# Where the two heads of a pair meet on TensorE: SSD products by head, or by pair of heads

## The chip, the cores and the metric

The kernel runs on one core of a Trainium2 chip. The metric is the device time of one execution in microseconds (us), as the median over runs. Three runs of the kernel before gave 815.00, 816.15 and 816.83 us, median 816.15 us.

## The reference

Two layers of a bidirectional hybrid encoder over 256 tokens of 1024 features, in float32. A layer projects the normalized input to the columns of two mixers: a Mamba-2 mixer (SSD, 16 heads of 64 features in 4 groups, two chunks of 128 tokens, run forward and backward) and a short gated convolution. Both outputs go through one output projection; then comes a gated MLP. The part that matters here is the chunked scan, once for each direction:

```python
scores = jnp.einsum('bclgn,bcsgn->bclsg', cm, bm)
y_diag = jnp.einsum('bclsgr,bcsgrp->bclgrp', scores[..., None] * decay_ls, xdt)
...
y_off = jnp.einsum('bclgn,bcgrpn->bclgrp', cm, h_prev) * jnp.exp(a_cs)[..., None]
return (y_diag + y_off).reshape(bsz, length, g, r, p)
```

`y_diag` is what each chunk adds to itself, head by head: a 128 x 128 matrix of weights times 64 features. `y_off` is what one chunk hands to the other.

## The kernel before

**Work and tiles.** All activations lie with 128 features on the partitions and 256 tokens along the row. A large weight matrix comes as a stream of 512 KB chunks (`issue`, L132): SyncE loads a chunk into `raw`, ScalarE rounds it to `wh` (L98), VectorE takes the rest as `wl` (L99), seven buffers each, four chunks ahead of use. `products` (L230) spends 24 TensorE products on a chunk: for four k tiles and two column tiles, weights times input in three parts. These products are the rows `mm<-nh,wh`, `mm<-nl,wh`, `mm<-nh,wl` of the trace (`mm<-mixh,wh` and so on in the output projection).

**The order on TensorE** is the order written in the code: the class `te` (L79) ties every product to the one before it. In a mixer's second half, `mixer` runs over twelve pairs of tiles of the short convolution's projection, `TRIPLES` (24 chunks), and then over the 16 chunks of the output projection, `OUT_ORDER`. Between chunks it slips in the work of the SSD. The chunks are counted as slots: n from 1 to 39. `HEADS_AT` (L47) says after which slot a head is begun: heads 0 to 15 after slots 1, 3, 3, 7, 9, 11, 11, 15, 17, 19, 19, 21, 21, 23, 24, 24.

**A head** (`head`, L471) is begun by ScalarE and VectorE, which make its 128 x 128 weights for both chunks, the tile `m` (five buffers, written last by VectorE at L487). `HEAD_LAG` = 4 slots later `products_of` (L544) is called through `run` (L538) and issues the head's products through `head_out` (L492):

- the head's own products, `py<-m,xt`: one for each chunk c, of the 64 columns of `xt` that belong to the head. An even head writes partitions 0 to 63 of the bank `py`, an odd head partitions 64 to 127. In the trace each of these float32 products is two rows, so a head has four;
- with an even head also `py<-so,xg`, one for each chunk, over all 128 columns, for both heads of the pair: four rows.

After an odd head VectorE takes the bank `py` out (L554 to L557: `yo`, then twice the tile `x`). After every fourth head the group is gated, squared and, four slots later, its norm is taken with one product `gt<-sq,ones` (`group_norm`, L566). Before the first head of a group, `group` (L445) issues four transposes `xp<-ident,x` and two products `sp<-C,B` (four rows each).

The rows of decays that a pair needs (`bc`, `er`) are fetched on GpSimd's queue (`load_rows`, L573). Banks `py`, `xp`, `sp`, `gt` share four PSUM buffers (`bank`, L175).

Of the kernel before, what the change touches and what calls it, by code (L numbers as in the profile page):

```python
# [16 lines left out]
P = 128  # L17
L = 256
# [11 lines left out]
# per-feature parameter columns: name -> (first column, columns)  # L30
# [7 lines left out]
# pairs of 128-column tiles of the input projection, in the order they are used  # L38
# [6 lines left out]
# heads of the SSD begun after a chunk of products, counted from the short conv's first  # L45
_STARTS = (1, 3, 3, 7, 9, 11, 11, 15, 17, 19, 19, 21, 21, 23, 24, 24)
HEADS_AT = {_n: _STARTS.count(_n) for _n in _STARTS}  # L47
HEAD_LAG = 4    # chunks from a head's weights to its products
NORM_LAG = 4    # chunks from a group's last products to its norm
ROWS_AHEAD = 2  # heads whose rows are fetched ahead  # L50
STAGES_AT = (3, 5, 7, 9)    # pairs of SILUS after which a stage of the discretisation follows
SPLIT_FROM = 7  # triple after which the outputs of the mixers are split
NORMS = {"n1": D, "n2": D, "fin": D, "gn": 2 * P}     # features under each mean
NU = 4           # pairs of a projection whose input is scaled by rstd only afterwards
LNEXP, SILU = "natural_log_exp_and_others", "silu_and_others"
AHEAD = 4        # chunks of weights split ahead of their use
WARM = 12       # products that raise the clock of TensorE
LAG = 6         # tiles of d_ff between the up and the down projection
TAIL = 4        # tiles of d_ff whose down projection runs output by output
# [3 lines left out]
def hybrid_trunk(ctx: ExitStack, tc: tile.TileContext, xT, w_in, w_dt, w_out, w_up, w_dn, w_dnt,  # L63
# [15 lines left out]
    class te:  # L79
        """TensorE in the order written here"""  # L80
# [51 lines left out]
    def issue(halves=1, between=lambda: None):  # L132
        src, kc, cols = plan[len(split)]
        n = kc * cols
        raw = wp.tile([P, KC * 256], F32, name="raw")
        wh = wp.tile([P, KC * 256], F32R, name="wh", bufs=7)
        if cols == 32:
            # both parts of a k tile side by side
            nc.sync.dma_start(out=raw[:, :n], in_=src)
            r3 = raw[:, :n].rearrange("p (k c) -> p k c", k=kc)  # L140
            w4 = wh[:, :2 * n].rearrange("p (k i c) -> p k i c", k=kc, i=2)
            hilo(r3, w4[:, :, 0, :], w4[:, :, 1, :])
            split.append((wh, None, kc, cols))
            return
        wl = wp.tile([P, KC * 256], F32R, name="wl", bufs=7)
        for i in range(halves):
            o = slice(i * n // halves, (i + 1) * n // halves)
            nc.sync.dma_start(out=raw[:, o], in_=src[:, o])
            hilo(raw[:, o], wh[:, o], wl[:, o])
            if i == 0:  # L150
                between()
        split.append((wh, wl, kc, cols))
# [44 lines left out]
    # TensorE's clock is raised while the first loads are under way  # L197
# [18 lines left out]
    def scaled(l):  # L216
        """the norms' weights over -2n, a power of two"""
        for i, (name, n) in enumerate(NORMS.items()):
            a = s.activation(wn[l][:, i], pars[l][:, COL[name]:COL[name] + 8], AF.Identity, scale=-0.5 / n)
            if l:  # L220
                after(a, tab["uses"][-1])
# [8 lines left out]
    def products(ps, wts, xs, first, last, js=None):  # L230
        """ps[:, j, :] += w[k, j]^T x[k] for the k of a chunk."""
        wh, wl, kc, cols = wts
        for kk in range(kc):
            xh, xl = xs[kk]
            for j in js or range(cols // P):
                o = kk * cols + j * P
                a, b = wh[:, o:o + P], wl[:, o:o + P]
                f = first and kk == 0
                e = last and kk == kc - 1
                te.matmul(ps[:, j, :], a, xh, start=f and j == 0, stop=False, skip_group_check=True)  # L240
                te.matmul(ps[:, j, :], a, xl, start=False, stop=False, skip_group_check=True)
                te.matmul(ps[:, j, :], b, xh, start=False, stop=e, skip_group_check=True)
# [10 lines left out]
    def squares(p, src, acc):  # L253
        """acc of the squares of the four pairs of h."""
# [13 lines left out]
    def rstd(sq, n, name, sq_on):  # L268
        """-2n / sqrt(mean + eps) over the features of a tile of squares, on all partitions"""
# [5 lines left out]
    def newton(tot, n, y, t, r, sq_on=s):  # L275
        """-2n / sqrt(tot/n + eps): the tables' value, and one step of Newton's"""
# [10 lines left out]
    def weighted(l, name):  # L287
        """h * w in two parts, pair by pair; the scaling by rstd follows the product."""
# [22 lines left out]
    def both(r):  # L311
        """[128, L] seen twice as [128, 2, L]"""
        return bass.AP(r.tensor, r.offset, [r.ap[0], [0, 2], r.ap[1]])

    class Norm:
        """The normalized input of a projection: h*w first, (h*w)*rstd once rstd is known."""
# [24 lines left out]
        def pairs(self, extra=None):  # L341
            """pair by pair; rstd is due after the first chunk of the second"""
# [19 lines left out]
    def discretise(l, nm):  # L362
        """softplus, decays and their prefix and suffix sums, rows of (chunk, head); then per token. In stages."""
# [49 lines left out]
        # what is left of the chunk after s (forward, chunk 0) and before s (backward, chunk 1)  # L413
        keep(s.activation(rows[1][64:96, :], cs[qd[0], :], AF.Identity, scale=-1.0, bias=cs[qd[0], P - 1:P]))
        keep(s.activation(rows[1][96:128, :], rs[qd[1], :], AF.Identity, scale=-1.0, bias=rs[qd[1], 0:1]))
        # the rows that every partition needs go through DRAM: [head, (cs forward, rs backward), token]
# [10 lines left out]
        # what a token adds to the other chunk: dt * exp(rest), [128, chunk, head]  # L427
# [6 lines left out]
        # the decay from the other chunk up to l: rows of chunk 0 (backward), of chunk 1 (forward)  # L434
# [8 lines left out]
    def diag(t):  # L443
        """of [128, 2 L] the blocks of the two chunks with themselves: [128, 2, 128]"""
        return bass.AP(t.tensor, t.offset, [t.ap[0], [3 * P, 2], [1, P]])  # L445
# [23 lines left out]
    def head(hd, bc, tok, grp):  # L469
# [10 lines left out]
        # of the two exponents the one that applies is not positive and the other not negative  # L480
# [9 lines left out]
    def head_out(hd, grp, m, py):  # L490
        """of two heads, what each chunk adds to itself, and to the other chunk without the decay up to l"""
        xt, _, so, xg = grp  # L492
        i, f = hd % 2, hd % HPG
        for c in range(2):
            te.matmul(py[64 * i:64 * i + 64, 0, c * P:(c + 1) * P], xt[:, c * L + f * 64:c * L + (f + 1) * 64],
                      m[:, c, :], start=True, stop=True, skip_group_check=True)
        if i == 0:
            for c in range(2):
                te.matmul(py[:, 1, (1 - c) * P:(2 - c) * P], xg[:, c, f:f + 2, :].rearrange("p f x -> p (f x)"),
                          so[:, c, :], start=True, stop=True, skip_group_check=True)  # L500

    def mixer(l):
# [35 lines left out]
        def run(slot):  # L538
            """what is due after a block of products of the projections"""
# [4 lines left out]
        def products_of(hd, grp, m):  # L544
            def f(slot):
                if hd % 2 == 0:
                    state["py"] = bank("py")
                py = state["py"]
                head_out(hd, grp, m, py)
                g, j = hd // HPG, (hd % HPG) // 2  # L550
                if hd % 2 == 1:
                    t = k1("yo")
                    er = state["er"].pop(0)
                    v.tensor_tensor(out=t, in0=py[:, 1, :], in1=er, op=ALU.mult)  # L554
                    v.scalar_tensor_tensor(out=xs[g][:, j, :], in0=xs[g][:, j, :], scalar=pc(l, "dsk", 2 * g + j),
                                           in1=py[:, 0, :], op0=ALU.mult, op1=ALU.add)
                    v.tensor_tensor(out=xs[g][:, j, :], in0=xs[g][:, j, :], in1=t, op=ALU.add)  # L557
# [15 lines left out]
        def load_rows(upto):  # L573
            """the rows of the next heads on all partitions, and of the pairs of heads on 64 partitions each"""
# [22 lines left out]
        def split_next():  # L597
            """the parts of the next tiles of the mixers' outputs that are ready, those first used first"""
# [7 lines left out]
        state.update(ready=[], rows=0, bc=[], er=[])  # L606
# [89 lines left out]
    final = {"turn": [], "hw": []}  # L696

    def turned(p):
        """h * w of a pair with the tokens on partitions: two pairs to a bank"""
# [31 lines left out]
# (output pair, quarter of K); the quarters run over the short-conv half first  # L731
# [3 lines left out]
# the down projection of a tile of d_ff LAG tiles behind its up projection  # L735
# [6 lines left out]
def _pairs(w, kt):  # L742
    """[K, 256 n] columns -> [n, 128, kt*256]: k on partitions, k tiles along the row."""
# [4 lines left out]
def _chunks(w, kt):  # L748
    """the same cut into chunks of KC k tiles: [n, kt/KC, 128, KC*256]"""
# [4 lines left out]
def _feat(a):  # L754
    """[..., n*128] -> [128, ... n] columns"""
# [50 lines left out]
```

## Time and profile before

| | |
|---|---|
| median of three runs | 816.15 us (815.00 to 816.83) |
| profiled execution, first to last instruction (span) | 813.0 us |
| TensorE busy in the span | 803.1 us (99%) |
| VectorE, ScalarE, GpSimd busy | 648.6 us (80%), 530.9 us (65%), 39.4 us (5%) |
| mean granted TensorE clock | 0.997 |
| mean DMA rate | 186 GB/s |

The profile gives the span alone as the profiled execution's own time: 813.0 us, which is 3.15 us under the median of the runs. Busy shares are averages over stages. The heads of the first layer lie between 95 and 190 us, those of the second between 490 and 585 us. In the rows, PE is TensorE's products, PEld its weight loads, DVE is VectorE, ACT is ScalarE, POOL is GpSimd. `128*64` in a row means 128 rows and 64 columns of the array.

### The profile page before, as it was taken

The numbers are of one execution on the slowest core, as the hardware profiler recorded it, in microseconds if no ns is written. First come the engines' busy times: TensorE is split into PE (matmuls) and PEld (weight loads), VectorE is DVE, ScalarE is ACT, GpSimd is POOL, SyncE is SP. The second block draws the span as 40 slices with busy tenths as digits, with TensorE's granted clock in tenths as the row PEclk, the third lists the DMA queues.
The fourth block names the chain that finished last, engine by engine and source line by source line (L and its number), as shares of the span: only waits on it lengthen the run. The fifth ranks groups of instructions, "written<-read, shape, count | busy, mean of one in ns | idle before, by whom it ended". The sixth has DMA issues, their size and how long they took to land.

```text
span 813.0 us, 16585 instructions
## 1 busy us (share of the span) xinstructions
PE 803.1 (99%) x6608; PEld 792.7 (98%) x6608; DVE 648.6 (80%) x1082; ACT 530.9 (65%) x940; POOL 39.4 (5%) x68
## 2 busy tenths in 40 slices
PE   8999999999999999999999999999999999999996
PEld 8999999999999999999999999999999999999996
DVE  6998788988799877776789768899878987767753
ACT  6777867974676555555667578789557655555543
POOL 1002211100000000000000202110000000000000
PEclk9999999999999999999999999999999999999998
DMA  8578667546536855554546767645564566656511
GB/s 277 185 241 289 177 233 210 182 123 221 181 115 179 252 182 184 181 183 162 183 154 190 232 225 215 206 157 181 172 195 154 151 208 216 183 183 182 184 44 52
DMA packets 46989, 150.89 MB, mean 186 GB/s; under 512 B 9136, under 2 KB 9712, under 8 KB 46912
## 3 DMA queue, kind: packets, MB, share of 16 engines
q1 hardware_dynamic: 38880, 138.17, 53.6%
q0 software_dynamic: 7456, 11.00, 4.5%
q8 instruction: 51, 0.84, 0.4%
q10 hardware_dynamic: 576, 0.68, 0.2%
q14 instruction: 26, 0.21, 0.1%
HBM read 148.62 MB, written 1.15 MB: 184 GB/s over the span
## 4 chain that ended last, share of the span: by engine, by line
PE 98%; DVE 1%; DMA 1%; ACT 0%; issue 0%; DVEq 0%; POOLq 0%
PE mm L91 76%; PE dn L91 16%; PE py L91 3%; PE sp L91 1%; DMA hp<-in_hpar_dram 1%; PE dtp L91 0%; PE xp L95 0%; PE gt L91 0%; DVE hwl L295 0%; PE tot L91 0%; PE mm L95 0%; DVE fo L726 0%; DVEq L802 0%; ACT sq L256 0%; ACT wh L98 0%
## 5 line engine op out<-in xcount | busy, mean ns | idle before, releaser
L98 ACT CAST wh<-raw 128x1024 fp32r<-128x1024 f32 (+1 forms) x264 | 272.5, 1035 | 228.0 <-PE mm L91 145.2
L99 DVE TENSOR_TENSOR wl<-raw,wh 128x1024 fp32r<-128x1024 f32 (+1 forms) x262 | 317.2, 1213 | 110.6 <-ACT wh L98 110.3
L91 PE MATMUL mm<-nh,wh 128*128 128x256 f32 x1216 | 346.6, 285 | 0.0
L91 PE MATMUL mm<-nl,wh 128*128 128x256 f32 x1216 | 344.0, 283 | 0.0
L91 PE MATMUL mm<-nh,wl 128*128 128x256 f32 x1216 | 344.0, 283 | 0.0
L91 PEld LDWEIGHTS mm<-nh,wh 128*128 128x128 f32 x1216 | 233.3, 192 | 0.9 <-issue 0.7
L91 PEld LDWEIGHTS mm<-nl,wh 128*128 128x128 f32 x1216 | 233.3, 192 | 0.2
L91 PEld LDWEIGHTS mm<-nh,wl 128*128 128x128 f32 x1216 | 233.3, 192 | 0.0
L91 PE MATMUL dn<-acth,wh 128*128 128x256 f32 x352 | 99.7, 283 | 0.0
L91 PE MATMUL dn<-acth,wl 128*128 128x256 f32 x352 | 99.6, 283 | 0.0
L91 PE MATMUL dn<-actl,wh 128*128 128x256 f32 x352 | 99.6, 283 | 0.0
L91 PE MATMUL mm<-hwh,wh 128*128 128x256 f32 x256 | 73.3, 286 | 1.1 <-ACT hwh L294 1.1
L91 PE MATMUL mm<-mixh,wh 128*128 128x256 f32 x256 | 73.9, 289 | 0.0
L91 PE MATMUL mm<-hwl,wh 128*128 128x256 f32 x256 | 72.5, 283 | 0.3 <-DVE hwl L295 0.3
L91 PE MATMUL mm<-mixl,wh 128*128 128x256 f32 x256 | 72.4, 283 | 0.0
L91 PE MATMUL mm<-hwh,wl 128*128 128x256 f32 x256 | 72.4, 283 | 0.0
L91 PE MATMUL mm<-mixh,wl 128*128 128x256 f32 x256 | 72.4, 283 | 0.0
L91 PEld LDWEIGHTS dn<-actl,wh 128*128 128x128 f32 x352 | 67.6, 192 | 0.0
L91 PEld LDWEIGHTS dn<-acth,wl 128*128 128x128 f32 x352 | 67.6, 192 | 0.0
L91 PEld LDWEIGHTS dn<-acth,wh 128*128 128x128 f32 x352 | 67.6, 192 | 0.0
L352 DVE SCALAR_TENSOR_TENSOR cacc<-mm,pars,cacc 128x255 f32<-128x255 f32 x96 | 45.6, 477 | 6.6 <-ACT cacc L351 6.6
L91 PEld LDWEIGHTS mm<-hwh,wh 128*128 128x128 f32 x256 | 49.0, 192 | 1.4 <-ACT hwh L294 1.3
(149 smaller groups left out, 1029.3 us busy)
## 6 DMA issues: line engine op xcount, KB each, us to landing
raw<-in_w_in_dram SPq DMA_DIRECT2D x94, 512.0 KB, 4.5
raw<-in_w_up_dram SPq DMA_DIRECT2D x88, 512.0 KB, 3.9
raw<-in_w_dn_dram SPq DMA_DIRECT2D x36, 512.0 KB, 3.7
raw<-in_w_out_dram SPq DMA_DIRECT2D x32, 512.0 KB, 4.0
bc<-dcs POOLq DMA_DIRECT2D x32, 256.0 KB, 5.2
raw<-in_w_dnt_dram SPq DMA_DIRECT2D x8, 512.0 KB, 3.6
er<-der POOLq DMA_DIRECT2D x16, 128.0 KB, 5.9
h<-in_xT_dram SPq DMA_DIRECT2D x4, 256.0 KB, 5.8
```

The lines of the kernel that those rows point to most:

```text
L91: cls.put(nc.tensor.matmul(*args, **kw))
L98: s.copy(hi, full)
L99: v.tensor_tensor(out=lo, in0=full, in1=hi.bitcast(F32), op=ALU.subtract)
L352: v.scalar_tensor_tensor(out=acc[:, 1:L], in0=u[:, 0:L - 1], scalar=w0, in1=acc[:, 1:L], op0=ALU.mult, op1=ALU.add)
```

## The change

`head_out` becomes `pair_out`. An even head's call of `products_of` now only keeps its weights `m`. The odd head's call issues the products of both heads: for each chunk c first the even head's (lower half of the columns), then the odd head's (upper half), and then the two products `py<-so,xg`. The bank `py` is taken at that moment, and no longer at the even head. Which products are made, their operands and their shapes stay the same, and so does all that VectorE, ScalarE and the queues are given to do. Lines below the change move by three (L554 becomes L557). Comments that the change also drops are left out here.

```diff
-    def head_out(hd, grp, m, py):
+    def pair_out(hd, grp, ms, py):
         xt, _, so, xg = grp
-        i, f = hd % 2, hd % HPG
-        for c in range(2):
-            te.matmul(py[64 * i:64 * i + 64, 0, c * P:(c + 1) * P], xt[:, c * L + f * 64:c * L + (f + 1) * 64],
-                      m[:, c, :], start=True, stop=True, skip_group_check=True)
-        if i == 0:
-            for c in range(2):
-                te.matmul(py[:, 1, (1 - c) * P:(2 - c) * P], xg[:, c, f:f + 2, :].rearrange("p f x -> p (f x)"),
-                          so[:, c, :], start=True, stop=True, skip_group_check=True)
+        f = hd % HPG
+        for c in range(2):
+            for i, m in enumerate(ms):
+                te.matmul(py[64 * i:64 * i + 64, 0, c * P:(c + 1) * P],
+                          xt[:, c * L + (f + i) * 64:c * L + (f + i + 1) * 64], m[:, c, :],
+                          start=True, stop=True, skip_group_check=True)
+        for c in range(2):
+            te.matmul(py[:, 1, (1 - c) * P:(2 - c) * P], xg[:, c, f:f + 2, :].rearrange("p f x -> p (f x)"),
+                      so[:, c, :], start=True, stop=True, skip_group_check=True)
...
         def products_of(hd, grp, m):
             def f(slot):
+                state["ms"].append(m)
                 if hd % 2 == 0:
-                    state["py"] = bank("py")
-                py = state["py"]
-                head_out(hd, grp, m, py)
+                    return
+                py = bank("py")
+                pair_out(hd - 1, grp, state["ms"], py)
+                state["ms"] = []
```

**How the order on TensorE moves.** First, in the first layer, the place where head 0's products stood, between two chunks' products (`mm`). A row `64x128 x2` is two products of 64 partitions by 128 tokens.

```order
 L91 MATMUL mm<-nl,wh 128x256
 L91 MATMUL mm<-nh,wl 128x256
-L91 MATMUL py<-m,xt 64x128 x2
-L91 MATMUL py<-so,xg 128x128 x2
 L91 MATMUL mm<-nh,wh 128x256
 L91 MATMUL mm<-nl,wh 128x256
```

Head 0's six products leave this place, and the two chunks' products now follow each other directly.

Second, two chunks later, on TensorE before the change. Here `m_1343` is head 1's weights and `m_1360` head 2's, `py_1433` is the bank of heads 0 and 1, `py_1508` that of heads 2 and 3.

```order
L91 MATMUL mm_1441<-nl_341,wh_1297 128x256
L91 MATMUL mm_1441<-nh_340,wl_1298 128x256
L91 MATMUL py_1433<-m_1343,xt_1238 64x128 x2
L91 MATMUL py_1508<-m_1360,xt_1238 64x128 x2
L91 MATMUL py_1508<-so_1244,xg_1248 128x128 x2
L91 MATMUL mm_1534<-nh_319,wh_1374 128x256
```

The same place with the change, where `m_1253` is head 0's weights, `m_1343` head 1's, and `py_1497` their bank.

```order
L91 MATMUL mm_1436<-nl_341,wh_1297 128x256
L91 MATMUL mm_1436<-nh_340,wl_1298 128x256
L91 MATMUL py_1497<-m_1253,xt_1238 64x128
L91 MATMUL py_1497<-m_1343,xt_1238 64x128
L91 MATMUL py_1497<-m_1253,xt_1238 64x128
L91 MATMUL py_1497<-m_1343,xt_1238 64x128
L91 MATMUL py_1497<-so_1244,xg_1248 128x128 x2
L91 MATMUL mm_1529<-nh_319,wh_1374 128x256
```

As many products stand here as before, but of heads 0 and 1 in place of 1 and 2, alternating between the halves, and all into one bank; before, the two halves went to two banks.

Third, the last pair of the first layer on TensorE before the change: `m_2430` is head 14's weights, `m_2445` head 15's.

```order
L91 MATMUL mm_2396<-mixh_2388,wl_2399 128x256
L91 MATMUL py_2601<-m_2430,xt_2251 64x128 x2
L91 MATMUL py_2601<-so_2257,xg_2261 128x128 x2
L91 MATMUL py_2601<-m_2445,xt_2251 64x128 x2
L91 MATMUL mm_2457<-mixh_2145,wh_2459 128x256
```

With the change (`m_2425` is head 14's, `m_2440` head 15's):

```order
L91 MATMUL mm_2391<-mixh_2383,wl_2394 128x256
L91 MATMUL py_2601<-m_2425,xt_2246 64x128
L91 MATMUL py_2601<-m_2440,xt_2246 64x128
L91 MATMUL py_2601<-m_2425,xt_2246 64x128
L91 MATMUL py_2601<-m_2440,xt_2246 64x128
L91 MATMUL py_2601<-so_2257,xg_2261 128x128 x2
L91 MATMUL mm_2452<-mixh_2145,wh_2454 128x256
```

Head 15's products move ahead of the two full-width ones.

On VectorE, the last of the five buffers of `m` to be taken again is the one of head 15, which head 10 held. Its place with the change:

```order
L485 SCALAR_TENSOR_TENSOR w_2439<-sm_2251,tok_1212,w_2439 128x128
L557 TENSOR_TENSOR yo_2490<-py_2483,er_2111 128x256
L485 SCALAR_TENSOR_TENSOR w_2439<-sm_2251,tok_1212,w_2439 128x128
L558 SCALAR_TENSOR_TENSOR x2_1064<-x2_1064,pars0_89,py_2483 128x256
L487 TENSOR_TENSOR m_2440<-e_2437,w_2439 128x256
```

`py_2483` is the bank of heads 10 and 11: its `yo` stands ahead of head 15's `m`, as it did before the change.

## Rows read from the trace of the kernel before

**Rows 1.** The page: span, busy shares, the clock over 40 slices, the chain that ended last.

```profile
span 813.0 us, 16585 instructions
PE 803.1 (99%) x6608; PEld 792.7 (98%) x6608; DVE 648.6 (80%) x1082; ACT 530.9 (65%) x940; POOL 39.4 (5%) x68
...
PEclk9999999999999999999999999999999999999998
...
PE 98%; DVE 1%; DMA 1%; ACT 0%; issue 0%; DVEq 0%; POOLq 0%
```

**Rows 2.** Waits of PE, the longest: us in total, times, longest.

```profile
PE mm L91 <- ACT hwh L294: 1.1, 1, 1.1
```

**Rows 3.** Timeline of PE, head 0: start, length (us), engine, line, operation, out<-in.

```profile
97.27 0.28 PE L91 MATMUL mm<-nh,wl 128*128 128x256 f32 x1
...
98.71 0.28 PE L91 MATMUL mm<-nh,wl 128*128 128x256 f32 x1
98.92 0.65 PE L91 MATMUL py<-m,xt 128*64 128x128 f32 x4
99.50 0.71 PE L91 MATMUL py<-so,xg 128*128 128x128 f32 x4
99.96 0.36 PE L91 MATMUL mm<-nh,wh 128*128 128x256 f32 x1
100.17 0.28 PE L91 MATMUL mm<-nl,wh 128*128 128x256 f32 x1
```

**Rows 4.** Timeline of PE, head 3 alone.

```profile
119.71 0.28 PE L91 MATMUL mm<-nh,wl 128*128 128x256 f32 x1
119.92 0.65 PE L91 MATMUL py<-m,xt 128*64 128x128 f32 x4
120.50 0.39 PE L91 MATMUL mm<-nh,wh 128*128 128x256 f32 x1
120.72 0.28 PE L91 MATMUL mm<-nl,wh 128*128 128x256 f32 x1
```

**Rows 5.** Timeline of PE, heads 1 and 2 together.

```profile
105.67 0.28 PE L91 MATMUL mm<-nh,wl 128*128 128x256 f32 x1
105.88 0.66 PE L91 MATMUL py<-m,xt 128*64 128x128 f32 x8
106.48 0.71 PE L91 MATMUL py<-so,xg 128*128 128x128 f32 x4
...
107.15 0.28 PE L91 MATMUL mm<-nl,wh 128*128 128x256 f32 x1
```

**Rows 6.** Timeline of PE, heads 14 and 15.

```profile
180.49 0.28 PE L91 MATMUL mm<-mixh,wl 128*128 128x256 f32 x1
180.70 0.65 PE L91 MATMUL py<-m,xt 128*64 128x128 f32 x4
...
181.92 0.65 PE L91 MATMUL py<-m,xt 128*64 128x128 f32 x4
...
182.72 0.28 PE L91 MATMUL mm<-mixl,wh 128*128 128x256 f32 x1
```

**Rows 7.** The tile py over the whole span: PE, then DVE's wait for it.

```profile
L91 PE MATMUL py<-m,xt x128: 272/273/323, 98.9 to 579.2; 128*64 128x128 f32 x128
...
DVE yo L554: 7.3, 6
```

**Rows 8.** Timeline of PE, group 1: products of the full array, without a head.

```profile
112.77 0.60 PE L95 MATMUL xp<-ident,x 128*128 128x128 f32 x4
113.21 1.03 PE L91 MATMUL sp<-C,B 128*128 128x256 f32 x4
```

**Rows 9.** Timeline of DVE: the weights m of heads 14 and 15.

```profile
174.14 0.42 DVE L487 TENSOR_TENSOR m<-e,w 128x256 f32<-128x256 f32 x1
...
175.72 0.42 DVE L487 TENSOR_TENSOR m<-e,w 128x256 f32<-128x256 f32 x1
```

**Rows 10.** Busy time of the engines in the stretch of the last heads: us, then PE, PEld, DVE, ACT, POOL.

```profile
155.00:190.00 35.00, 35.00 (x284) 33.13 (x284) 32.01 (x68) 26.51 (x60) 1.36 (x2) 1.00 0.51 161
```

More of the change, by code (lines that the diff above doesn't have):

```diff
@@ L545, in f @@
             def f(slot):
+                state["ms"].append(m)
                 if hd % 2 == 0:
-                    state["py"] = bank("py")
-                py = state["py"]
-                head_out(hd, grp, m, py)
+                    return
+                py = bank("py")
+                pair_out(hd - 1, grp, state["ms"], py)
+                state["ms"] = []
                 g, j = hd // HPG, (hd % HPG) // 2
[L551 to L557, printed above, removed]
+                t = k1("yo")
+                er = state["er"].pop(0)
+                v.tensor_tensor(out=t, in0=py[:, 1, :], in1=er, op=ALU.mult)
+                v.scalar_tensor_tensor(out=xs[g][:, j, :], in0=xs[g][:, j, :], scalar=pc(l, "dsk", 2 * g + j),
+                                       in1=py[:, 0, :], op0=ALU.mult, op1=ALU.add)
+                v.tensor_tensor(out=xs[g][:, j, :], in0=xs[g][:, j, :], in1=t, op=ALU.add)
                 if hd % HPG == HPG - 1:
@@ L604, in split_next @@
                     mix[k + j] = (hi[:, j, :], lo[:, j, :])
-        state.update(ready=[], rows=0, bc=[], er=[])
+        state.update(ready=[], rows=0, bc=[], er=[], ms=[])
         cur = {}
```

## The prediction

> **What bounds the kernel now.** Read the page first. TensorE is busy for 803.1 of 813.0 us and carries 98% of the chain that ended last, at the full granted clock in every slice but the last [rows 1]. Of all its waits for other engines the longest sum is 1.1 us, one wait for the first normalized input [rows 2]; none is for a head's weights. So the time is the length of TensorE's own stream, and an edit to that stream is worth what it takes out of it, as long as nobody else becomes late. Next comes the timeline of TensorE, and there the distance between starts rather than the length of a row, since products overlap in their pipe. In a plain run of chunk products twelve steps take 98.71 - 97.27 = 1.44 us, 0.12 each [rows 3]. A visit to a head is therefore measured from the last chunk product ahead of it to the second one behind it, less two plain steps (0.24 us).
>
> **What a visit costs.** Four kinds stand in the trace, each priced so:
> - an even head alone, with its two full-width products: 100.17 - 98.71 - 0.24 = 1.22 us [rows 3];
> - an odd head alone: 120.72 - 119.71 - 0.24 = 0.77 us [rows 4];
> - an odd head and the next pair's even head in the same visit: 107.15 - 105.67 - 0.24 = 1.24 us [rows 5];
> - heads 14 and 15, with the full-width products between them: 182.72 - 180.49 - 0.24 = 1.99 us [rows 6].
>
> The third row is the one to look at. Eight rows of 64 columns last 0.66 us there, against 0.65 us for four in rows 3 and 4. The upper half's products (head 1) and the lower half's (head 2) run beside each other, and the second head is nearly free: 1.24 against 1.22 us. The single products say what else is in a visit. Four full-array rows of 128 tokens need 113.21 - 112.77 = 0.44 us [rows 8]; an odd head alone has four rows too and costs 0.77, so going into the 64-column form and out again costs 0.33 us.
>
> **The change part by part.** By the table of starts, before the change a layer has three visits of the first kind (heads 0, 4, 8), three of the second (3, 7, 13), four of the third (1 with 2, 5 with 6, 9 with 10, 11 with 12) and the last one. That is 3 x 1.22 + 3 x 0.77 + 4 x 1.24 + 1.99 = 3.66 + 2.31 + 4.96 + 1.99 = 12.92 us. With the change a layer has eight visits, one for each pair, and each holds eight 64-column rows and four full-width ones, as many and of the same forms as the third kind. At 1.24 us they cost 9.92. **A layer saves 3.00 us, two layers 6.0.** Nothing is removed from the count of products: 128 rows of 64 columns (32 heads by four, the first at 98.9 us and the last at 579.2 us [rows 7]) stay 128. What goes is time between them. Of the twelve times that a layer enters the 64-column form (the last visit enters it twice) four go, 4 x (0.33 + 0.44) = 3.1 us, which agrees.
>
> One thing the trace of before does not show: in its shared visits the two halves write two banks, and now they write one, in alternation. From below this costs nothing more than rows 5, and a gain is excluded: each half still has a chain of four rows. From above it costs the whole overlap: eight rows one after the other, 4 x 0.11 = 0.44 us more for a pair. I take nothing, because rows 5 are the same instructions on the same two halves, and the two halves of a bank lie on different partitions.
>
> How the hardware treats the order is the second question. In rows 5 the program issues all four rows of the upper half first, and the eight still end 0.01 us later than four. So a row of one half does not wait for earlier rows of the other half. The Trainium skill says otherwise: by "TensorE: Matmul & The Clock Gate", section "The mechanism", matmuls start and end strictly in program order and only weight loads are pulled ahead. By that rule the sum would be 4.2 us, as under the first rival below; rows 5 disagree with it, and by them the sum stays 6.0.
>
> What moves with the change. **The even heads wait** up to four slots longer for their products, and their `m` stays in its buffer for so long. The tightest reuse is head 15's, of head 10's buffer; VectorE's `yo` of heads 10 and 11 stands ahead of that write in its queue before and after, so no wait is added. **VectorE's `yo`** after an odd head now follows the full-width products too (99.50 to 99.96, 0.46 us later [rows 3]) in four visits of a layer. I cost it at nothing: what stands behind it on VectorE has a lead over TensorE, below, and that lead covers it. **TensorE comes early** to the later heads, most at the end of a layer: by 3.00 - (1.99 - 1.24) = 2.25 us at heads 14 and 15. It would want them at 180.70 - 2.25 = 178.45 us; head 15's `m` is written at 175.72 + 0.42 = 176.14 [rows 9]. So 2.3 us are left even if VectorE gets no faster, and it does where it waits for `py` (7.3 us in all [rows 7]). The fetches on GpSimd's queue and the weight stream on SyncE's keep their order; no queue is passed by anything.
>
> **The sum.** The profiled execution's span goes from 813.0 to 807.0 us. The median of the runs is 3.15 us above that span, which I leave as it is: 816.15 - 6.0 = **810.1 us**, 0.74% less.
>
> **The rivals.**
> 1. The halves overlap, but only in program order. For a pair the eight rows come as two of the lower half, two of the upper, and again; the two of a half follow each other, and only the seams between halves overlap. Five row times in place of four, 0.11 us more for a pair, 16 x 0.11 = 1.8 us: 811.9 us. Against it: rows 5 would then need seven row times, and show four. Chance 0.06.
> 2. Two halves in one bank exclude each other. 16 x 0.44 = 7.0 us more: 817.2 us, which is no difference that can be measured (0.2%, 1.6 us, is about what a measurement of this kernel tells from none). For it: no row of before has both halves in one bank. Against it: the partitions are different. The skill's "TensorEngine Tiling (Array Packing)", section "Gotcha 1: PSUM Pressure", states such a rule for row tiles, which these are not; no run here shows it. Chance 0.03.
> 3. **Slower:** each change from one half to the other empties the array, as a change of form does. The place is the alternation inside a pair: three such changes, each at half of the 0.33 us for in and out, 0.50 us, and no overlap, 0.44 us; 16 x 0.94 = 15.0 us against 6.0 saved: 825.2 us. It decides the sign once a pair's eight rows take over 6.0 / 16 = 0.38 us longer than the 0.66 of rows 5. Against it: rows 5 hold such neighbours and show no such cost. Chance 0.03.
> 4. VectorE becomes late. In the stretch of the last heads it is busy 32.01 of 35 us [rows 10], and TensorE asks 2.25 us earlier. If its weights fell 4 us behind, the lead of 2.3 would not cover 1.7 us in a layer, 3.4 in both: 813.5 us. Against it: the lead above. Chance 0.04.
>
> **How the numbers follow.** The forecast has 0.84 and gives the time, 810.1 us. Around it lie the spread of runs (815.00 to 816.83, 0.9 to each side) and reading starts to 0.01 us (about 0.2), so 809.0 to 811.2; I add 0.4 below for the spread of a three-run median seen again. Upwards the range takes in the first rival with half of that spread, 811.9 + 0.6. That is **808.6 to 812.5**; the other rivals, 0.10 together, and what noise leaves are outside. Faster by over 0.2% are the forecast and rivals 1 and 4: 0.94. Within 0.2% is rival 2: 0.03. Slower by over 0.2% is rival 3: 0.03.
>
> **What would show it.** In the changed kernel's timeline each layer should have eight visits with rows `py<-m,xt` x8 of 0.66 us followed by `py<-so,xg` x4, and no `x4` of the 64-column form; from the last chunk product to the second after it 1.48 us. A row x8 of 0.77 us speaks for rival 1, of 1.1 us for rival 2, of 1.6 us for rival 3. The waits of TensorE should stay at those of before; a wait of `py` for VectorE's `m` at L487 in the later heads speaks for rival 4. The prediction is wrong if the visits cost 1.24 us and the time is still above 812.5: then what TensorE gave up returned elsewhere, as a wait in the output projection behind the heads.

## The result, and the profile after

With the change the median of four runs is **810.41 us** (809.56 to 811.60), beside 816.08 us (815.00 to 816.83, four runs) for the kernel before. The ratio is 0.9933, 95% interval 0.9919 to 0.9947. Forecast were 810.1 us and a ratio of 0.9926.

The page of the kernel after, in the lines that answer to [rows 1]:

```profile
span 809.5 us, 16577 instructions
PE 798.9 (99%) x6608; PEld 790.9 (98%) x6608; DVE 648.2 (80%) x1082; ACT 530.1 (65%) x940; POOL 39.3 (5%) x68
...
PEclk8999999999999999999999999999999999999998
...
PE 98%; DMA 1%; ACT 0%; DVE 0%; issue 0%; DVEq 0%; POOLq 0%
```

TensorE has the same 6608 products, is still the chain, and its stream is shorter. But the span fell by 3.5 us alone. Two things hide in that. The profiled run is the slowest of the four (811.6 us), and its first slice shows an 8 for the granted clock, where before stands a 9. So compare stretches that begin and end at the same product of the program. The product `tot` closes each norm; the first of a layer stands ahead of that layer's heads, the second behind them. Its rows on TensorE's timeline, before:

```profile
19.14 0.59 PE L91 MATMUL tot<-sqh,ones 128*128 128x256 f32 x2
...
223.73 0.59 PE L91 MATMUL tot<-sqh,ones 128*128 128x256 f32 x2
...
416.08 0.59 PE L91 MATMUL tot<-sqh,ones 128*128 128x256 f32 x2
...
620.67 0.59 PE L91 MATMUL tot<-sqh,ones 128*128 128x256 f32 x2
```

And after:

```profile
21.78 0.59 PE L91 MATMUL tot<-sqh,ones 128*128 128x256 f32 x2
...
223.31 0.59 PE L91 MATMUL tot<-sqh,ones 128*128 128x256 f32 x2
...
415.65 0.59 PE L91 MATMUL tot<-sqh,ones 128*128 128x256 f32 x2
...
617.18 0.59 PE L91 MATMUL tot<-sqh,ones 128*128 128x256 f32 x2
```

The first layer's stretch went from 204.59 to 201.53 us, the second's from 204.59 to 201.53 as well: **3.06 us for a layer**, 6.12 in all. Between the layers 192.35 us became 192.34. All of the gain lies where the heads are. The 2.64 us that the span lost lie ahead of the first `tot` (19.14 against 21.78 us) and belong to the start of that one execution, not to the heads; the last section looks at them.

The visit to heads 0 and 1 on TensorE's timeline after, which answers to [rows 5]:

```profile
107.11 0.28 PE L91 MATMUL mm<-nh,wl 128*128 128x256 f32 x1
107.32 0.66 PE L91 MATMUL py<-m,xt 128*64 128x128 f32 x8
107.91 0.71 PE L91 MATMUL py<-so,xg 128*128 128x128 f32 x4
108.37 0.36 PE L91 MATMUL mm<-nh,wh 128*128 128x256 f32 x1
108.58 0.28 PE L91 MATMUL mm<-nl,wh 128*128 128x256 f32 x1
```

From the last chunk product to the second after it 1.47 us, less 0.24: the visit costs 1.23 us. The other fifteen visits read the same, those with a norm's product `gt` ahead of them included, once that product's own time is taken off.

The waits of TensorE after, the longest, which answers to [rows 2]:

```profile
PE mm L91 <- ACT hwh L294: 2.4, 1, 2.4
```

It is again the one wait for the first weighted input; none is for `m`.

VectorE and TensorE at the last pair of the second layer, after (VectorE's row is `m` of head 15, which answers to [rows 9]):

```profile
569.48 0.42 DVE L487 TENSOR_TENSOR m<-e,w 128x256 f32<-128x256 f32 x1
...
574.91 0.66 PE L91 MATMUL py<-m,xt 128*64 128x128 f32 x8
```

The weights are ready 574.91 - 569.90 = 5.0 us ahead. VectorE's wait for `py` fell from 7.3 us [rows 7] to 1.0 us in the view of that tile:

```profile
DVE yo L557: 1.0, 4
```

### The profile page after: what moved, and what is told of

Read it like the earlier page. It is cut to its first block, busy times and chain, and to the rows that moved or that the text cites. A ratio compares the mean times of both kernels' runs of the same rounds, so it can differ in the third digit from the quotient of the medians.

```text
span 809.5 us, 16577 instructions
## 1 busy us (share of the span) xinstructions
PE 798.9 (99%) x6608; PEld 790.9 (98%) x6608; DVE 648.2 (80%) x1082; ACT 530.1 (65%) x940; POOL 39.3 (5%) x68
## 4 chain that ended last, share of the span: by engine, by line
PE 98%; DMA 1%; ACT 0%; DVE 0%; issue 0%; DVEq 0%; POOLq 0%
PE mm L91 77%; PE dn L91 16%; PE py L91 2%; PE sp L91 1%; DMA hp<-in_hpar_dram 1%; PE dtp L91 1%; PE xp L95 0%; PE gt L91 0%; PE tot L91 0%; PE mm L95 0%; DVE fo L729 0%; DVEq L805 0%; ACT sq L256 0%; ACT wh L98 0%; DVE hwl L295 0%
## 5 line engine op out<-in xcount | busy, mean ns | idle before, releaser
L91 PEld LDWEIGHTS mm<-hwl,wh 128*128 128x128 f32 x256 | 50.1, 196 | 0.5 <-DVE hwl L295 0.4
```

The costliest lines, as they stand in the source:

```text
L91: cls.put(nc.tensor.matmul(*args, **kw))
```

## The experiments

The theory: what the change saves is time between TensorE's products, because a pair's eight 64-column rows always run two by two on the two halves, and because the array enters the 64-column form eight times in a layer and not twelve. The rivals are those of the prediction. Five runs, each an edit of the kernel after.

**e1_grouped: the order inside a pair.** The pair stays in one visit, but head by head.

```diff
-        for c in range(2):
-            for i, m in enumerate(ms):
+        for i, m in enumerate(ms):
+            for c in range(2):
```

> As the change, but a pair's products are issued head by head: all of the lower half, then all of the upper half. Theory (each half has its own stream, whatever the order in the program): a visit stays at 1.23 to 1.24 us, the eight rows at 0.66 us, and the time at 810.4 us, as with the change (within 1 us). Rival (rows start in the order of the program, only the seam overlaps): seven row times in place of four, 0.33 us more for a pair, 16 x 0.33 = 5.2 us, 815.6 us. Rival (it is the alternation that brings the gain): the same side, a visit near 1.6 us.

Measured: 810.02 us (ratio to before 0.9928, 0.9913 to 0.9942). The same visit on TensorE's timeline:

```profile
105.63 0.28 PE L91 MATMUL mm<-nh,wl 128*128 128x256 f32 x1
105.84 0.66 PE L91 MATMUL py<-m,xt 128*64 128x128 f32 x8
...
107.11 0.28 PE L91 MATMUL mm<-nl,wh 128*128 128x256 f32 x1
```

1.48 - 0.24 = 1.24 us, eight rows in 0.66 us. The alternation that the change writes out is of no account; that the two heads are neighbours is. A row of the second head does not wait until the four rows of the first have started: with that wait the eight would need seven row steps of 0.11 us, and they need four. The Trainium skill's rule that matmuls start strictly in program order ("TensorE: Matmul & The Clock Gate", section "The mechanism") does not hold for two halves of the array in this kernel: by it these eight rows would take three row times more, 0.99 us.

**e2_full_between: one visit, no neighbours.**

```diff
-        for c in range(2):
-            for i, m in enumerate(ms):
+        for i, m in enumerate(ms):
+            for c in range(2):
                 te.matmul(py[64 * i:64 * i + 64, 0, c * P:(c + 1) * P],
                           xt[:, c * L + (f + i) * 64:c * L + (f + i + 1) * 64], m[:, c, :],
                           start=True, stop=True, skip_group_check=True)
-        for c in range(2):
-            te.matmul(py[:, 1, (1 - c) * P:(2 - c) * P], xg[:, c, f:f + 2, :].rearrange("p f x -> p (f x)"),
-                      so[:, c, :], start=True, stop=True, skip_group_check=True)
+            if i == 0:
+                for c in range(2):
+                    te.matmul(py[:, 1, (1 - c) * P:(2 - c) * P], xg[:, c, f:f + 2, :].rearrange("p f x -> p (f x)"),
+                              so[:, c, :], start=True, stop=True, skip_group_check=True)
```

> As the change, with one visit for a pair, but the two full-width products stand between the two heads' products, as they stood for heads 14 and 15 before. Theory (what is saved is the overlap of neighbours on the two halves and the entries into the 64-column form): every visit costs 1.99 us, as the last one of a layer did before, 16 x (1.99 - 1.23) = 12.2 us more than the change, 822.6 us, which is slower than before. Rival (the gain comes from fewer visits between the chunks' products, and the order inside one is of no account): 810.4 us.

Measured: 822.04 us (ratio to before 1.0071, 1.0054 to 1.0088). TensorE's timeline:

```profile
105.59 0.28 PE L91 MATMUL mm<-nh,wl 128*128 128x256 f32 x1
105.80 0.65 PE L91 MATMUL py<-m,xt 128*64 128x128 f32 x4
106.38 0.71 PE L91 MATMUL py<-so,xg 128*128 128x128 f32 x4
107.03 0.65 PE L91 MATMUL py<-m,xt 128*64 128x128 f32 x4
...
107.83 0.28 PE L91 MATMUL mm<-nl,wh 128*128 128x256 f32 x1
```

The visit costs 2.24 - 0.24 = 2.00 us, as heads 14 and 15 did [rows 6]. Eight visits of this kind are slower than the eleven of before. So fewer visits as such bring nothing: the same products in the same slots win 6 us or lose 6, by whether four full-width rows stand between the halves. The two effects come together here: such a visit has no overlap, and it enters the 64-column form twice. e3 and e4 take them apart.

**e3_one_half: neighbours, but on one half.** Both heads write the lower half, one after the other; VectorE takes the full-width products' sums in their place, so the heads' own products are left out of the output.

```diff
-                te.matmul(py[64 * i:64 * i + 64, 0, c * P:(c + 1) * P],
+                te.matmul(py[0:64, 0, c * P:(c + 1) * P],
...
-                                       in1=py[:, 0, :], op0=ALU.mult, op1=ALU.add)
+                                       in1=py[:, 1, :], op0=ALU.mult, op1=ALU.add)
```

> As the change, but both heads write the lower half of the columns, so that the odd head's sums replace the even head's; VectorE takes the full-width products' sums in place of them, in an operation of the same shape (the heads' own products are left out of the output). Theory (the two halves are what lets eight rows take the time of four): eight rows one after the other, 4 x 0.11 = 0.44 us more for a pair, a visit at 1.67 us, 16 x 0.44 = 7.0 us more than the change, 817.4 us. Rival (rows of 64 columns overlap wherever they lie): 810.4 us.

Measured: 816.54 us (ratio to before 1.0007, 0.9998 to 1.0016). TensorE's timeline:

```profile
105.29 0.28 PE L91 MATMUL mm<-nh,wl 128*128 128x256 f32 x1
105.50 1.09 PE L91 MATMUL py<-m,xt 128*64 128x128 f32 x8
...
107.18 0.28 PE L91 MATMUL mm<-nl,wh 128*128 128x256 f32 x1
```

Eight rows take 1.09 us in place of 0.66, the visit 1.89 - 0.24 = 1.65. The whole gain is gone with the second half, and nothing but the half, and with it the place in the bank that the odd head writes, is changed in those products. The place alone does not explain it: a single head's four rows write two places of one half and need 0.65 us as well [rows 4]. This is also the size that the second rival had named for two halves that shut each other out of one bank; the change itself, at 0.66 us, shows that they don't.

**e4_four_heads: the price of entering the form.** All four heads of a group in one visit, with the same alternation; eight buffers of `m` and four of `er` hold what waits.

```diff
-        m = tmp.tile([P, 2, P], F32, name="m", bufs=5)
+        m = tmp.tile([P, 2, P], F32, name="m", bufs=8)
...
             for i, m in enumerate(ms):
-                te.matmul(py[64 * i:64 * i + 64, 0, c * P:(c + 1) * P],
-                          xt[:, c * L + (f + i) * 64:c * L + (f + i + 1) * 64], m[:, c, :],
+                te.matmul(pys[i // 2][64 * (i % 2):64 * (i % 2) + 64, 0, c * P:(c + 1) * P],
+                          xt[:, c * L + i * 64:c * L + (i + 1) * 64], m[:, c, :],
...
-                if hd % 2 == 0:
+                if hd % HPG < HPG - 1:
                     return
-                py = bank("py")
-                pair_out(hd - 1, grp, state["ms"], py)
+                pys = [bank("py"), bank("py")]
+                pair_out(hd, grp, state["ms"], pys)
...
```

> All four heads of a group in one visit after the last of them: 16 rows of 64 columns, alternating, then 8 full-width ones; eight buffers for m and four for er. Theory (going into the 64-column form and out costs 0.33 us for a visit): four visits in a layer in place of eight, each at two pairs' 2.46 less 0.33 us, 8 x 0.33 = 2.6 us less than the change, 807.8 us. Rival (a longer visit and later banks make VectorE or the norms late, or the entry's price is a matter of the rows and not of the form): 810.4 us or more, with waits of TensorE for m or sq.

Measured: 807.13 us (ratio to before 0.9894, 0.9879 to 0.9908). TensorE's timeline:

```profile
117.97 0.28 PE L91 MATMUL mm<-nh,wl 128*128 128x256 f32 x1
118.18 1.09 PE L91 MATMUL py<-m,xt 128*64 128x128 f32 x16
119.20 1.16 PE L91 MATMUL py<-so,xg 128*128 128x128 f32 x8
...
120.32 0.28 PE L91 MATMUL mm<-nl,wh 128*128 128x256 f32 x1
```

The visit costs 2.35 - 0.24 = 2.11 us where two pairs cost 2.46: 0.35 us for one entry saved, against 0.33 worked out ahead. Eight of them are 2.8 us; the medians are 3.3 us apart. TensorE waits for no `m` and no `sq` here. This version is faster than both kernels.

Is it the form that costs, or any visit between two chunks' products? The trace of before has a visit without a 64-column row, the transposes and products of group 1 [rows 8]. The chunk products around it:

```profile
112.65 0.28 PE L91 MATMUL mm<-nh,wl 128*128 128x256 f32 x1
...
114.19 0.28 PE L91 MATMUL mm<-nl,wh 128*128 128x256 f32 x1
```

It costs 1.54 - 0.24 = 1.30 us for four rows of 128 tokens and four of 256. At 0.11 us for every 128 tokens the rows alone are 1.32 us, so this visit pays nothing beyond them. And in e2 the odd head's rows follow full-width rows of the same visit, and still add 2.00 - 1.22 = 0.78 us [rows 3], about as much as an odd head alone, 0.77 [rows 4]. The price belongs to the 64-column form.

**e5_lag2: the cover.** Products two chunks, not four, behind the weights.

```diff
-HEAD_LAG = 4
+HEAD_LAG = 2
```

> As the change, with two chunks in place of four from a head's weights to its products (HEAD_LAG 2). With the change head 15's m is written 5.0 us ahead of its products, head 1's 5.1, head 13's 5.3, the other odd heads' 6 to 9; two chunks are 5.8 us. Theory (the four chunks of lag are the cover that hides VectorE's making of m): TensorE begins to wait for m, at heads 1, 13 and 15, 0.5 to 0.8 us each, up to 2 us in a layer: 811 to 814.5 us, with waits of py for VectorE in the trace. Rival (VectorE's pace follows TensorE's and the weights simply come earlier too): no waits, 810.4 us.

Measured: 814.19 us (ratio to before 0.9983, 0.9973 to 0.9992). The waits of TensorE, and two visits of the first layer, heads 0 and 1, then 10 and 11:

```profile
PE py L91 <- DVE m L487: 1.4, 3, 0.8
```

```profile
99.91 0.43 PE L91 MATMUL py<-m,xt 128*64 128x128 f32 x2
100.66 0.65 PE L91 MATMUL py<-m,xt 128*64 128x128 f32 x6 [0.32 <-DVE m L487]
...
163.81 0.43 PE L91 MATMUL py<-m,xt 128*64 128x128 f32 x2
165.01 0.65 PE L91 MATMUL py<-m,xt 128*64 128x128 f32 x6 [0.77 <-DVE m L487]
```

The even head's first product goes, then TensorE stands until VectorE has the odd head's `m`. The eight rows end at 101.31 and 165.66 us, 1.40 and 1.85 us after they began, not 0.66. The 1.4 us in the list of waits are three gaps alone, and less than what was lost, as the stretches below show. So the lag is what hides VectorE, and two chunks of it are not enough: by the medians 3.8 of the 5.7 us are given back. Late were heads 1, 7, 11 and 15, not quite the ones expected (1, 13, 15). In the first layer their `m` was written 0.7, 0.4, 1.2 and 0.1 us after the pair's first product had begun, so head 11, which had not been expected, was the latest: with the lag the order on VectorE changes too, and the leads read at lag 4 only say that the cover is thin, not where it tears first.

**The same runs without their starts.** The medians hold the start of the kernel, which differs from run to run (last section). Between the two `tot` of a layer, where the change takes 201.53 us, e1 takes 201.57, e2 207.63, e3 204.97 us in either layer, e4 200.17 and 200.18, and e5 204.15 and 203.47. For both layers, against the change, e2 loses 12.2 us (12.2 were expected), e3 6.9 (7.0), e4 wins 2.7 (2.6), and e5 loses 4.6 (up to 4): 2.6 in the first layer, where at most 2 had been expected, and 1.9 in the second.

## Why the prediction was right

**What bounds the kernel** held: TensorE is the chain before and after, and what was taken out of its stream came out of the time.

**The price of a visit** held to 0.01 us. Taken were 1.24 us, from the shared visits of before; measured were 1.23. For a layer 3.00 us were forecast, from starts read to 0.01 us, and 3.06 measured; for the kernel 6.0 and, by the medians, 5.7, with 6.1 in the trace's two stretches. The span that the forecast named on the way, 807.0 us, did not come: the profiled execution's was 809.5, and those of the four runs 807.8 to 809.5. In these four runs the time lies 1.8 to 2.1 us above the run's own span, so about 1 us of the 3.15 us that the sum carried over stood for something else: the execution profiled before was a short one (813.0 us, where others of that kernel had up to 815.3). The forecast of the time is not touched by it, since the saving was taken off the median itself.

**The unknown,** two halves in one bank and in alternation, cost nothing, the lower of the two bounds. e1 and the change differ by 0.01 us in a visit.

**The two parts of the saving** were each tested alone: the overlap (e3: without it 1.65 in place of 1.23, 0.42 us for a pair, forecast 0.44) and the entry into the form (e4: 0.35 us, forecast 0.33). The Trainium skill says the same of the second: changing the tiling mode, not just the tile, drains the engine ("TensorEngine Tiling (Array Packing)", section "Key Properties"); the trace agrees, with 0.33 to 0.35 us for in and out and nothing for a change of half. What the engine does in that time the trace does not show.

**The rivals.** Program order (811.9 us): refuted by the rows of the change, 0.66 us for eight, and by e1, where it would have cost most. Halves that exclude each other in a bank, and a drain at each change of half: refuted by the same 0.66 us. VectorE late: it did not happen. There the prediction was too careful. It left head 15 a lead of 2.3 us, on the ground that VectorE might get no faster; measured were 5.0 in both layers. Ahead of the change the lead was 181.92 - 176.14 = 5.8 [rows 6, 9]. TensorE came to head 15's products 2.25 us earlier by the sum, and 1.22 more because they now stand first in the visit (181.92 - 180.70), 3.5 in all; the lead shrank by 0.8, so VectorE came 2.7 us earlier. Its waits for `py` shrank by 6.3 us, which fits, though no run shows that this alone is the reason. e5 shows that the danger was real all the same, with 5.0 us in hand where two chunks are 5.8.

## What to carry to other kernels

Where a product uses half of the array's columns, put its counterpart for the other half directly next to it: in this kernel the second head then costs 0.01 us, in whatever order the rows of the two are issued. On the same half it costs 0.43, and with four full-width rows between the two heads 0.78. Enter such a form seldom, as each visit pays 0.33 to 0.35 us beyond its rows; four heads to a visit were better than two. Price a visit by the starts of the plain products around it, and look in the trace of before for a place where two neighbours already stand together: it gives the price of the change without a model.

## What the runs showed that was not expected

The start of the kernel moved the span by 2.6 us between the two profiled executions, close to half of what the change saves. The stretch ahead of 15 us, before and after (us, then busy time of PE, PEld, DVE, ACT, POOL, then the granted clock):

```profile
0.00:15.00 15.00, 12.19 (x78) 11.58 (x79) 7.94 (x18) 10.44 (x24) 2.52 (x8) 1.00 0.84 290
```

```profile
0.00:15.00 15.00, 11.44 (x56) 10.85 (x57) 7.60 (x18) 10.01 (x22) 2.52 (x8) 0.77 0.81 278
```

The granted clock of the stretch is given as 1.00 (2.4 GHz) before, and as 0.77 after, where part of it runs at the lower level of 1.2 GHz. On TensorE's timeline before, the products `warm`, which the kernel issues ahead of everything else, then the first chunk's first product:

```profile
1.05 5.29 PE L91 MATMUL warm<-ones 128*128 128x128 f32 x24 [1.05 <-DVE eps L202]
7.46 0.38 PE L91 MATMUL mm<-hwh,wh 128*128 128x256 f32 x1 [1.11 <-ACT hwh L294]
```

The same after, and the steps that follow:

```profile
1.06 4.54 PE L91 MATMUL warm<-ones 128*128 128x128 f32 x24 [1.06 <-DVE eps L202]
7.97 0.58 PE L91 MATMUL mm<-hwh,wh 128*128 128x256 f32 x1 [2.38 <-ACT hwh L294]
...
9.27 0.41 PE L91 MATMUL mm<-hwh,wh 128*128 128x256 f32 x1
9.48 0.41 PE L91 MATMUL mm<-hwl,wh 128*128 128x256 f32 x1
```

Read the clock of the view with the rows beside it: before, too, the 24 rows of `warm` take 0.22 us each, where a row of this form takes 0.11 later [rows 8], though the view says 1.00. After, TensorE was idle for 2.38 us ahead of the first input, in place of 1.11: `warm` was through 0.74 us earlier, and the input came 0.51 us later. TensorE came back at steps of 0.21 us in place of 0.12. The change touches nothing there. The four runs' spans were 807.8, 807.9, 809.1 and 809.5 us, with mean clocks of 0.996, 0.995, 0.992 and 0.992: the longer spans have the lower clock. The idle time alone does not decide it. In e1 TensorE waited 1.1 us for the first input, as before, and the granted clock of the same stretch was 0.89 all the same:

```profile
PE mm L91 <- ACT hwh L294: 1.1, 1, 1.1
```

```profile
0.00:15.00 15.00, 12.49 (x68) 11.97 (x69) 7.68 (x17) 9.85 (x21) 2.52 (x8) 0.89 0.82 278
```

Why the clock falls in one execution and not in another, and why the first input comes later in some, was not tried and stays open.
